# Four gate projections moved between the head pairs, five latent projections moved beside the triangular inverse

## The chip, the core and the metric

The kernel runs on one core of a Trainium2 chip. The metric is the device time of one execution in microseconds (us); lower is better. The engines are named as in the profile: PE is the matrix engine (PEld its weight loads, which overlap with it), DVE the vector engine, ACT the scalar engine, POOL the general engine, SP the engine that issues nearly all DMAs here. Every engine works off its own instructions in a fixed order; semaphores tie the orders together.

## What is computed

One layer of an encoder over 784 tokens (16 shared meta tokens, a prompt of 512 and a sample of 256). After a layer norm, one input projection feeds two branches; their outputs are concatenated, projected, normed, and put through a feed-forward block of width 4096.

```python
proj = h @ w_in                      # 1024 features -> 22 tiles of 128 columns
c_q, c_kv, k_r, qkv, z, a_f, a_b, b_f, b_b = split(proj)
q = rms_norm(c_q) @ w_uq             # latents of the attention: c_q 384, c_kv 256 columns
k, v = rms_norm(c_kv) @ w_uk, rms_norm(c_kv) @ w_uv
mla_out = softmax_attention(q, k, v)
qkv = silu(conv4(qkv))               # gated delta rule, both directions, 8 heads
m = strictly_lower((k*beta) @ k.T * decay)          # per chunk of 64 tokens
sol = solve(m + eye, ...)            # unit triangular, 112 matrices
o = scan over chunks (state S);  o = rms_norm(o) * silu(z)     # z: the gate, 512 columns
h = layer_norm(alpha*h + concat(mla_out, o) @ w_out)
h = layer_norm(alpha*h + relu(h @ w_ff1)**2 @ w_ff2)
```

## The kernel before

**Input projection.** `proj(ti)` makes one tile of 128 projected columns for all tokens. It loads 512 KB of weights (`wr`), splits them into a rounded part and a rest (`wh` by ACT, `wl` by DVE or POOL, chosen by `eng`), and issues 48 matmuls (8 feature tiles, 3 products, 2 halves of the tokens, 384 or 400 wide) into one of the two double banks `d2` of PSUM (`bank2()`). The weight tiles have two buffers each. There are 22 tiles: 0 holds the rotary keys and the decay gates; 1 to 8 are k and q of the four head pairs, in turns; 9 to 12 are v; 13 to 16 are the output gate z; 17 and 18 are the latents of k and v, 19 to 21 those of q.

**Pair stage.** `for j in range(NPB)` takes the four pairs in turn. `conv` projects k, then q, copies the result to `xb` and convolves it back into the same PSUM double bank (`y = ps...` where `wi < 8`). It stays there until `silu_pad` reads it with Silu. Then come the norms `l2` (Ln, Exp), the transposes `tokens`, the decay matrices `dc` and `en` (loads `x3` from `gD`, Exp), and the products that fill `LT` and the DRAM tile `UD`. ACT has to change its table between Silu and Ln/Exp. `act` puts the table load in place and orders it in the source's order: a load comes after every earlier activation of the other set. So pair j+1's Silu comes after all of pair j's Ln and Exp, and pair j+1's Ln after its own k's and q's Silu.

**First inverse.** `LT` is transposed (L585) and copied by DVE to `LP` (L587). `inv_steps` (L596, L598) then does 30 dependent steps of two DVE instructions each. The loop at L714 puts four such steps ahead of each of the eight tiles v0 to v3 (`vtok`) and z0 to z3 (`zgate`). `zgate` projects, applies Silu from PSUM to an SBUF tile, and stores that to `zD`; nobody reads `zD` before `finish`, in the delta rule. v is convolved into SBUF.

**Second inverse, latents, delta rule, attention.** The rest of the inverse (L724 to L775) ends in the stores to `tD`. Then `lat()` is a generator: its first part projects the five latent tiles and norms those of k and v, its next 18 parts are the up-projections (L657, L680, L704), one of them for each unit of the delta rule's loop (L904). Attention, output projection and feed-forward follow. Attention's pools and PSUM tiles lie where the inverse's and `lat()`'s lay, so it begins after both.

The framework's planner fixes every engine's order ahead of time. It runs the program through a model of the chip and gives an engine the earliest instruction in the source that is ready by that model; so later work moves ahead into idle places as far as its buffers are free, and the order doesn't change on the chip.

Of the kernel before, what the change touches and what calls it, by code (L numbers as in the profile page):

```python
# [5 lines left out]
F32 = mybir.dt.float32  # L6
# [10 lines left out]
NT = NM + NA + NB          # 784 unique tokens  # L17
NR = NA + NB               # 768 real tokens
KT = D // P                # 8 feature tiles
HT = NT // 2               # 392  # L20
HR = NR // 2               # 384
H0 = NT - HR               # 400
NCH = 14                   # 64-token chunks: A meta, A x8, B meta, B x4
GC = NCH * 64              # 896
NPB = 4                    # head pairs
# [59 lines left out]
def lay(inp):  # L85
    """host side: only places the inputs."""
    a = {}
    a["x"] = np.concatenate([inp["meta_tokens"], inp["x_prompt"][0], inp["x_sample"][0]], 0)
    w = inp["w_in"][0]
    cq, ckv, kr, q, k, v, z, g = (np.s_[0:384], np.s_[384:640], np.s_[640:672], np.s_[672:1184],  # L90
                                  np.s_[1184:1696], np.s_[1696:2208], np.s_[2208:2720], np.s_[2720:2752])
    tiles = [np.concatenate([w[:, kr], w[:, kr], w[:, g], np.zeros((D, 32), w.dtype)], 1)]
    for j in range(4):
        tiles.append(w[:, k][:, j * 128:(j + 1) * 128])
        tiles.append(w[:, q][:, j * 128:(j + 1) * 128])
    for s in (v, z, ckv, cq):
        t = w[:, s]
        for j in range(t.shape[1] // 128):
            tiles.append(t[:, j * 128:(j + 1) * 128])
    # [tile, p, k, 128]  # L100
    a["w_in"] = np.stack([t.reshape(KT, P, 128).transpose(1, 0, 2) for t in tiles])
    cols = [inp["ln_in_g"].reshape(8, 128).T, inp["ln_in_b"].reshape(8, 128).T]
    cols.append(inp["ln1_g"][0].reshape(8, 128).T)
    cols.append(inp["ln1_b"][0].reshape(8, 128).T)
    cols.append(inp["g_cq"][0].reshape(3, 128).T)
    cols.append(inp["g_ckv"][0].reshape(2, 128).T)
    cols.append(np.tile(inp["gdn_norm_g"][0], 2)[:, None])
    cols.append(inp["conv_w"][0].reshape(4, 12, 128).transpose(2, 1, 0).reshape(128, 48))
    a["cols"] = np.concatenate(cols, 1)
    a["gates"] = np.concatenate([inp["a_log_f"][0], inp["a_log_b"][0], inp["dt_bias_f"][0], inp["dt_bias_b"][0]])[None]  # L110
    a["rows"] = np.stack([inp["ln_in_g"], inp["ln_in_b"], inp["ln1_g"][0], inp["ln1_b"][0], inp["ln2_g"][0], inp["ln2_b"][0]])
    u = inp["w_uq"][0].reshape(384, 8, 96)
    t = []
    for h in range(8):
        n, r = u[:, h, :64], u[:, h, 64:]
        sw = np.concatenate([r[:, 16:], r[:, :16]], 1)
        t.append(np.concatenate([n, r, sw] if h % 2 == 0 else [r, sw, n], 1))
    a["w_uq"] = np.stack([x.reshape(3, 128, 128).transpose(1, 0, 2) for x in t], 1)   # [p, h, 3, 128]
    a["w_uk"] = inp["w_uk"][0].reshape(2, 128, 512).transpose(1, 0, 2)
    a["w_uv"] = inp["w_uv"][0].reshape(2, 128, 512).transpose(1, 0, 2)  # L120
    a["w_out"] = inp["w_out"][0]
    a["w_ff1"] = inp["w_ff1"][0].reshape(KT, P, FF // P, P).transpose(2, 1, 0, 3)    # [ft, p, k, 128]
    a["w_ff2"] = inp["w_ff2"][0]
    a["consts"] = _C
    a["rope"] = rope_tables()
    return {n: np.ascontiguousarray(v) for n, v in a.items()}
# [11 lines left out]
def body(ctx, tc, I, O):  # L138
# [10 lines left out]
    def banks_set(**bufs):  # L149
        """the eight banks, cut anew: name=number of tiles, of two banks where the name ends in 2."""  # L150
        want = list(bufs.items())
        n = 0
        while n < min(len(cut), len(want)) and cut[n][0] == want[n]:
            n += 1
        while len(cut) > n:
            (m, _), es = cut.pop()
            es.close()
            del banks[m]
        for m, b in want[n:]:
            es = ExitStack()  # L160
            banks[m] = es.enter_context(tc.tile_pool(name=f"ps_{m}", bufs=b, space=PSUM, reuse_waits="tile"))
            cut.append(((m, b), es))
# [15 lines left out]
    # activation table sets, switched in groups  # L178
# [31 lines left out]
    def split(src, hi, lo, eng=None):  # L210
        """hi + lo = src."""
        S.copy(hi, src)  # L212
        return (eng or V).tensor_sub(lo, src, hi.bitcast(F32))  # L213
# [3 lines left out]
    def moments(x, n, out, sp_):  # L217
        """mean and variance of the rows of x."""
# [5 lines left out]
    def norm_factors(m2, mv, sp_):  # L224
        """mv[..., 0] = -mean * rstd, mv[..., 1] = rstd from the mean and variance in m2[..., 2]."""
# [35 lines left out]
    bds = []  # L261
    for i in range(2):
        b = cvp.tile([P, 7, P], F32, name=f"bd{i}")
        G.memset(b, 0.0)
        bds.append(b)
# [54 lines left out]
    def proj(ti, real=False, wr=None, eng=V):  # L320
        """psum halves of projection tile ti: tokens 0..399 (16..399) and 400..783."""
# [71 lines left out]
    # gathered to [(h', s), dir, tile, parity, pair]  # L393
# [15 lines left out]
    # rows of gc (both directions) and -beta (forward), one line per (h', pair, chunk)  # L409
# [14 lines left out]
    egk = gqp.tile([P, 2, NCH, 4], F32, name="egk")      # exp(gc)  # L424
    act(egk, gcT, AF.Exp)
    ekd = gqp.tile([P, 2, NCH, 4], F32, name="ekd")      # exp(gl - gc)
    V.tensor_sub(ekd, glT, gcT)
    act(ekd, ekd, AF.Exp)
    egl = gqp.tile([P, 2, NCH, 4], F32, name="egl")      # exp(gl), natural head order
# [3 lines left out]
    # rotated keys, common to the heads  # L433
# [9 lines left out]
    ltp = pool(ctx, "ltp", 1, "left")  # L443
    LT = ltp.tile([P, 2, 56, 64], F32, name="LT")
    UD = dp.tile([2, NCH, P, 4, 2, 64], F32, name="UD")     # q, attention of a chunk
    vD = dp.tile([NCH, P, 4, 2, 64], F32, name="vD")        # k, v
# [5 lines left out]
    def conv(ti, wi, eng=V, ceng=V):  # L452
        """convolved projection tile (before silu), [128, 803]: A at 0, B at 531."""
# [19 lines left out]
    sp = pool(es, "sp", 1)  # L473

# [27 lines left out]
    def tokens(src, kt, j, w, mk):  # L502
        """src [(head, channel), chunks] by tokens to field w of the pair's k, v."""
# [21 lines left out]
    for j in range(NPB):  # L525
# [7 lines left out]
        for half in range(2):  # L533
# [3 lines left out]
            # rows of gc (both directions), -beta; of gc with the heads swapped  # L537
# [6 lines left out]
            # -beta decay, decay (forward); -beta decay, decay (backward)  # L544
# [13 lines left out]
            for a, w in ((0, 4), (4, 3)):  # L558
# [11 lines left out]
                for r in range(2):  # L570
                    st(UD[r, n0 + a:n0 + a + w, :, j].rearrange("n p i c -> p n (i c)"), ua[:, r, :w].rearrange("p n i c -> p n (i c)"))
    es.close()
    vp = pool(ec, "vp", 1)

    ei = ExitStack()
    ip = pool(ei, "ip", 1, "left")
# [24 lines left out]
    def lat():  # L601
# [1 line left out]
        def latent(t0, n, real, width, gn):  # L603
            cuts = ((NM if real else 0, H0), (H0, NT))
            a0 = cuts[0][0]
            raw = []
            sq = ml.tile([P, NT], F32, name="lsq")
            for i in range(n):
                ps = proj(t0 + i, real=real, eng=(V, V, V, G, G)[t0 + i - 17])
                r = ml.tile([P, NT], F32, name="lr", bufs=3)  # L610
                for s, (c0, c1) in enumerate(cuts):
                    S.copy(r[:, c0:c1], ps[:, s, :c1 - c0])
                if i == 0:
                    S.activation(sq[:, a0:], r[:, a0:], AF.Square)
                else:
                    s2 = ml.tile([P, NT], F32, name="ev", bufs=2)
                    S.activation(s2[:, a0:], r[:, a0:], AF.Square)
                    G.tensor_add(sq[:, a0:], sq[:, a0:], s2[:, a0:])
                raw.append(r)
            yield None  # L620
# [12 lines left out]
            yield res  # L633
# [10 lines left out]
        lk, lq = latent(17, 2, False, 256, "gckv"), latent(19, 3, True, 384, "gcq")  # L644
        next(lk)
        ck = next(lk)
        next(lq)
        yield
        halves = ((0, H0), (H0, NT))
# [42 lines left out]
        cq = next(lq)  # L692
        tq = ml.tile([P, NT], F32, name="lr", bufs=3)[:, :NR]
# [20 lines left out]
    for j in range(2 * NPB):  # L714
# [4 lines left out]
        else:  # L719
            zgate(j - NPB)  # L720
# [20 lines left out]
    for n0, r in ((0, 0), (96, 1), (16, 0), (80, 1), (32, 0), (64, 1), (48, 0), (56, 1)):  # L741
# [33 lines left out]
        st(tD.rearrange("p d n j c -> p (d n j) c")[:, ns], LTn[:, ns])  # L775
    el2 = ExitStack()
    ml = pool(el2, "ml", 1, "left")
    mv_ = pool(el2, "mv", 1, "left")
    latg = lat()
    next(latg)  # L780
    e1.close()

    # the chunk matrices are in DRAM by now: their place serves again
# [30 lines left out]
    def unit_a(c, step):  # L814
# [8 lines left out]
        # k exp(gc), v; q, attention, exp(gl), k exp(gl - gc)  # L823
# [107 lines left out]
    ei.close()  # L931
# [132 lines left out]
    def h1_half(s):  # L1064
        """normed tokens of one half, transposed; then scaled by rows for the residual."""
# [139 lines left out]
```

## Time and profile before

| | |
|---|---|
| median of 3 runs | 1242.83 us (1242.46 to 1246.13) |
| span of the profiled execution | 1241.3 us |
| instructions | 18703 |
| PE busy | 1168.4 us, 94% |
| DVE busy | 717.2 us, 58% |
| ACT busy | 511.2 us, 41% |
| POOL busy | 171.8 us, 14% |
| mean granted TensorE clock | 0.973 of full speed |

The span is the time from the first to the last instruction of one execution; the median of the runs lies 1.5 us above it. Busy shares are averages over stages with quite different limits, so the stages have to be read one at a time.

### The profile page before, as it was taken

Reading aid. Unit: us, or ns where it says so; the run is one execution under the profiler, and the core shown is the slowest. Engines: PE = TensorE matmul, PEld = TensorE weight load, DVE = VectorE, ACT = ScalarE, POOL = GpSimd, SP = SyncE. Lnnn points to the kernel's source line nnn. Section 1 sums busy time; section 2 is a strip of 40 time slices with the busy share of each in tenths; the row PEclk is TensorE's granted clock in tenths of the full one; section 3 lists DMA queues with packets and bytes.
Section 4 is the critical chain, followed back from the end, with each engine's and each line's share of the span. In section 5 each row is a group of like instructions: output and inputs, shape, how many; then the busy total and the mean of one; then the engine's idle time right before and its main releaser. Section 6 shows DMA issues by size and latency. Waiting matters only on the chain.

```text
span 1241.3 us, 18703 instructions
## 1 busy us (share of the span) xinstructions
PE 1168.4 (94%) x7468; PEld 1021.7 (82%) x7468; DVE 717.2 (58%) x1136; ACT 511.2 (41%) x974; POOL 171.8 (14%) x201
## 2 busy tenths in 40 slices
PE   5978879998999999989999899999999999999995
PEld 4867879998889877756758798989898989899994
DVE  8567668697967867684456584334243424343348
ACT  5475655324645666563545521203030303121113
POOL 2144554024223221020100000000000000000000
PEclk9888899999999999999999899999999999999998
DMA  5147764522497845340210230303030303131002
GB/s 202 50 111 182 183 166 142 122 92 90 143 268 220 250 132 137 124 140 31 93 52 35 85 102 30 106 24 114 1 119 17 119 18 102 35 100 36 1 1 102
DMA packets 92202, 126.49 MB, mean 102 GB/s; under 512 B 34946, under 2 KB 63362, under 8 KB 92114
## 3 DMA queue, kind: packets, MB, share of 16 engines
q1 hardware_dynamic: 92114, 125.28, 33.9%
q8 instruction: 59, 0.97, 0.3%
q14 instruction: 29, 0.24, 0.1%
HBM read 98.73 MB, written 26.53 MB: 101 GB/s over the span
## 4 chain that ended last, share of the span: by engine, by line
PE 78%; DVE 9%; DMA 5%; ACT 3%; issue 2%; SPq 1%; POOL 1%; DVEq 0%; ACTq 0%; POOLq 0%
PE d L1061 21%; PE b L1167 21%; PE d L331 7%; PE b L1103 5%; DMA x<-gD 3%; PE v L1000 3%; PE c L1003 3%; PE d L969 3%; PE d L704 2%; PE b L837 2%; PE b L853 2%; PE b L877 2%; PE b L870 2%; DVE LP L598 1%; DVE tm L596 1%
## 5 line engine op out<-in xcount | busy, mean ns | idle before, releaser
L1061 PE MATMUL d<-h1h,w1h 128*128 128x384 f32 x512 | 171.5, 337 | 1.3 <-ACT LT L1142 1.3
L1061 PE MATMUL d<-h1l,w1h 128*128 128x384 f32 x512 | 172.0, 336 | 0.0
L1061 PE MATMUL d<-h1h,w1l 128*128 128x384 f32 x512 | 171.9, 336 | 0.0
L1167 PE MATMUL b<-w2l,fh 128*128 128x512 f32 x384 | 151.3, 394 | 0.0
L1167 PE MATMUL b<-w2h,fh 128*128 128x512 f32 x384 | 150.5, 392 | 0.0
L1167 PE MATMUL b<-w2h,fl 128*128 128x512 f32 x384 | 147.6, 389 | 0.0
L1171 DVE TENSOR_TENSOR acc<-acc,b 128x512 f32<-128x512 f32 x84 | 55.9, 685 | 137.9 <-PE b L1167 137.9
L331 PE MATMUL d<-hTh,wl 128*128 128x384 f32 (+1 forms) x352 | 124.7, 354 | 4.2 <-DVE wl L213 4.2
L331 PE MATMUL d<-hTh,wh 128*128 128x384 f32 (+1 forms) x352 | 125.5, 356 | 2.1 <-ACT ks L188 2.1
L212 ACT CAST w2h<-LT 128x1024 fp32r<-128x1024 f32 x32 | 31.9, 1045 | 230.9 <-PE b L1167 212.3
L331 PE MATMUL d<-hTl,wh 128*128 128x384 f32 (+1 forms) x352 | 125.9, 358 | 0.1
L1061 PEld LDWEIGHTS d<-h1h,w1h 128*128 128x128 f32 x512 | 96.3, 189 | 2.7 <-ACT LT L1142 1.6
L1061 PEld LDWEIGHTS d<-h1l,w1h 128*128 128x128 f32 x512 | 96.7, 189 | 0.9 <-DVE h1l L213 0.3
L1061 PEld LDWEIGHTS d<-h1h,w1l 128*128 128x128 f32 x512 | 96.7, 189 | 0.6 <-DVE w1l L213 0.3
L213 DVE TENSOR_TENSOR w1l<-LT,w1h 128x1024 fp32r<-128x1024 f32 x32 | 39.2, 1224 | 88.9 <-ACT w1h L212 88.7
L1167 PEld LDWEIGHTS b<-w2h,fl 128*128 128x128 f32 x384 | 72.1, 188 | 16.1
L1167 PEld LDWEIGHTS b<-w2h,fh 128*128 128x128 f32 x384 | 72.1, 188 | 15.9
L1167 PEld LDWEIGHTS b<-w2l,fh 128*128 128x128 f32 x384 | 72.2, 188 | 13.7
L212 ACT CAST w1h<-LT 128x1024 fp32r<-128x1024 f32 x32 | 33.5, 1050 | 100.3 <-PE d L1061 100.2
L331 PEld LDWEIGHTS d<-hTh,wl 128*128 128x128 f32 x352 | 68.3, 194 | 6.7 <-DVE wl L213 4.6
L331 PEld LDWEIGHTS d<-hTh,wh 128*128 128x128 f32 x352 | 68.1, 193 | 6.7 <-issue 3.4
L331 PEld LDWEIGHTS d<-hTl,wh 128*128 128x128 f32 x352 | 68.1, 193 | 2.9 <-issue 1.5
(316 smaller groups left out, 2265.6 us busy)
## 6 DMA issues: line engine op xcount, KB each, us to landing
LT<-in_w_ff SPq DMA_DIRECT2D x64, 512.0 KB, 3.3
wr<-in_w_in SPq DMA_DIRECT2D x22, 512.0 KB, 3.3
x<-gD SPq DMA_DIRECT2D x16, 560.0 KB, 5.6
KV<-vD SPq DMA_DIRECT2D x26, 256.0 KB, 4.4
U<-UD SPq DMA_DIRECT2D x26, 256.0 KB, 5.2
UD<-ua SPq DMA_DIRECT2D x16, 256.0 KB, 5.1
wor<-in_w_out SPq DMA_DIRECT2D x8, 512.0 KB, 6.5
TB<-tD SPq DMA_DIRECT2D x52, 64.0 KB, 2.5
```

The costliest lines, as they stand in the source:

```text
L212: S.copy(hi, src)
L213: return (eng or V).tensor_sub(lo, src, hi.bitcast(F32))
L331: T.matmul(ps[:, s, :c1 - c0], lhsT=a[:, k, :], rhs=b[:, k, c0:c1], start=(k == 0 and i == 0), stop=(k == KT - 1 and i == 2))
L704: T.matmul(ps[:, s, :HR], lhsT=a[:, k], rhs=b[:, cs], start=(k == 0 and i == 0), stop=(k == 2 and i == 2))
L837: T.matmul(ps[:, j * P:(j + 1) * P], lhsT=TB[:, j], rhs=KV[:, j], start=True, stop=True)
L969: T.matmul(ps[:, :w], lhsT=q[:, qs], rhs=kt[:, k0:k0 + w], start=True, stop=True)
L1000: T.matmul(ps[:, t * P:(t + 1) * P], lhsT=p[:, c0:c0 + P], rhs=dg, start=True, stop=True)
L1003: T.matmul(po[:m, :nq], lhsT=Vs[j][:, t0 + bi, :m], rhs=pt[:, :nq], start=(bi == 0), stop=(bi == ntl - 1))
L1061: T.matmul(ps[:, s, :HR], lhsT=a[:, k, :], rhs=b[:, k, s * HR:(s + 1) * HR], start=(k == 0 and i == 0), stop=(k == KT - 1 and i == 2))
L1103: T.matmul(ps, lhsT=x[:, k, :], rhs=y[:, cs], start=(k == 0 and i == 0), stop=(k == 3 and i == 2))
L1167: T.matmul(ps, lhsT=a[:, qs], rhs=b[:, cs], start=(f == 0 and i == 0), stop=(f == NG - 1 and i == 2))
L1171: V.tensor_add(acc[:, ti, cs], acc[:, ti, cs], ps)
```

## The change

Besides removed comments the diff does four things. `zgate(j)` is called at the end of each pair's turn. The projections of the five latent tiles leave `lat()` and become `latraw(i)`, called in the loop of the first inverse after the four v tiles, where z stood; their raw results and sums of squares get tiles of their own (`lraw`, `lsqs`), which live until the up-projections end. `lat()`'s pools move to the right side of SBUF, opened after the projection's tiles (`hTh`, `hTl`, the weights) are given back, and the inverse's own pool is given back before `lat()` starts. The block matrices `bds` move to the pair stage's pool.

```diff
-    bds = []                                   # in pool cvp
+    bds = []                                   # the same, in pool sp
...
                     st(UD[r, n0 + a:n0 + a + w, :, j]...)
+        zgate(j)
     es.close()
     vp = pool(ec, "vp", 1)

+    elr = ExitStack()
+    lrp = pool(elr, "lrp", 1, "left")
+    lraw = [lrp.tile([P, NT], F32, name=f"lr{i}") for i in range(5)]
+    lsqs = [lrp.tile([P, NT], F32, name=f"lsq{i}") for i in range(2)]
+    def latraw(i):
+        real = i >= 2
+        ps = proj(17 + i, real=real, eng=(V, V, V, G, G)[i])
+        r, sq = lraw[i], lsqs[real]
+        a0 = NM if real else 0
+        for s, (c0, c1) in enumerate(RHALVES if real else HALVES):
+            S.copy(r[:, c0:c1], ps[:, s, :c1 - c0])
+        if i in (0, 2):
+            S.activation(sq[:, a0:], r[:, a0:], AF.Square)
+        else:
+            s2 = ytile()[:, :NT]
+            S.activation(s2[:, a0:], r[:, a0:], AF.Square)
+            G.tensor_add(sq[:, a0:], sq[:, a0:], s2[:, a0:])
...
         def latent(t0, n, real, width, gn):
-            raw = []
-            sq = ml.tile([P, NT], F32, name="lsq")
-            for i in range(n):
-                ps = proj(t0 + i, real=real, ...)    # and copy, square, add
-            yield None
+            raw = lraw[t0:t0 + n]
+            sq = lsqs[real]
...
-        lk, lq = latent(17, 2, False, 256, "gckv"), latent(19, 3, True, 384, "gcq")
-        next(lk)
-        ck = next(lk)
-        next(lq)
+        ck = latent(0, 2, False, 256, "gckv")
         yield
...
-        cq = next(lq)
-        tq = ml.tile([P, NT], F32, name="lr", bufs=3)[:, :NR]
+        cq = latent(2, 3, True, 384, "gcq")
+        tq = ml.tile([P, NT], F32, name="tq")[:, :NR]
...
-    for j in range(2 * NPB):
+    for j in range(NPB + 5):
         for _ in range(4):
             next(gi, None)
         if j < NPB:
             vtok(j)
         else:
-            zgate(j - NPB)
+            latraw(j - NPB)
...
+    e1.close()
     el2 = ExitStack()
-    ml = pool(el2, "ml", 1, "left")
-    mv_ = pool(el2, "mv", 1, "left")
+    ml = pool(el2, "ml", 1)
+    mv_ = pool(el2, "mv", 1)
+    ei.close()
     latg = lat()
     next(latg)
-    e1.close()
...
     el2.close()
-    ei.close()
+    elr.close()
```

## Rows read from the trace of the kernel before

**Rows 1.** Busy time by stretch: engines, granted clock, DMA share, GB/s.

```profile
60.00:205.00 145.00, 122.67 (x637) 112.42 (x636) 101.49 (x115) 90.40 (x156) 73.83 (x57) 0.89 0.64 156
205.00:302.30 97.30, 94.01 (x558) 92.81 (x556) 79.55 (x99) 34.81 (x57) 18.81 (x30) 1.00 0.36 97
302.30:360.00 57.70, 52.87 (x1110) 48.71 (x1111) 39.77 (x57) 35.81 (x61) 20.33 (x33) 0.91 0.59 193
360.00:647.00 287.00, 280.23 (x2032) 212.88 (x2030) 189.82 (x401) 166.08 (x430) 47.76 (x55) 0.99 0.47 138
647.00:1241.00 594.00, 573.70 (x2880) 517.28 (x2880) 266.17 (x377) 153.79 (x206) 0.00 (x0) 0.99 0.18 61
```

**Rows 2.** Timeline of ACT, table loads and Silu: start, us, instruction, [idle before].

```profile
68.01 1.28 ACT L184 ACT_TABLE_LOAD   x1
...
88.28 1.28 ACT L184 ACT_TABLE_LOAD   x1
89.57 0.90 ACT L188 ACTIVATE ks<-d 128x528 f32<-128x528 f32 x2
...
105.50 0.90 ACT L188 ACTIVATE ks<-d 128x528 f32<-128x528 f32 x2 [11.96 <-DVE d L465]
106.41 1.28 ACT L184 ACT_TABLE_LOAD   x1
...
126.86 1.28 ACT L184 ACT_TABLE_LOAD   x1
128.15 0.90 ACT L188 ACTIVATE ks<-d 128x528 f32<-128x528 f32 x2
131.70 0.90 ACT L188 ACTIVATE ks<-d 128x528 f32<-128x528 f32 x2 [2.65 <-DVE d L465]
132.62 1.28 ACT L184 ACT_TABLE_LOAD   x1
...
155.35 1.28 ACT L184 ACT_TABLE_LOAD   x1
...
170.86 1.28 ACT L184 ACT_TABLE_LOAD   x1
...
193.86 1.28 ACT L184 ACT_TABLE_LOAD   x1
```

**Rows 3.** Waits from 60 to 205 us: total, times, longest.

```profile
DVE dc L547 <- DMA x<-gD: 23.0, 7, 6.4
...
PE b L507 <- ACT kt L508: 7.2, 2, 4.6
```

**Rows 4.** The chain that ended last, 60 to 330 us: a projection run.

```profile
242.39 20.08 PE d L331 x113
```

**Rows 5.** Timeline of ACT, the steps from a projected tile to its Silu (q0).

```profile
61.67 0.48 ACT L457 COPY xb<-d 128x400 f32<-128x400 f32 x1
...
62.84 0.94 ACT L462 ACTIVATE d<-xb,cols 128x803 f32<-128x803 f32 x1
...
67.09 0.90 ACT L188 ACTIVATE ks<-d 128x528 f32<-128x528 f32 x2 [1.95 <-DVE d L465]
```

**Rows 6.** Stores of z, over the whole span.

```profile
L523 SPq DMA_DIRECT2D zD<-y x4: 320/326/568, 227.7 to 255.7; - x4
```

**Rows 7.** Timeline of DVE: last product into LT, first and last inverse step.

```profile
204.31 0.55 DVE L566 TENSOR_TENSOR LT<-b,dc 128x384 f32<-128x384 f32 x1
...
230.92 0.38 DVE L596 TENSOR_TENSOR tm<-LP 112x120 f32<-112x120 f32 x1
...
301.99 0.28 DVE L598 TENSOR_TENSOR LP<-LP,tm 112x120 f32<-112x120 f32 x1
```

**Rows 8.** Line L704 alone, by stretch: PE and PEld busy, clock, DMA.

```profile
360.00:400.00 40.00, 22.49 (x110) 18.29 (x108) 1.00 0.86 238
```

**Rows 9.** Instructions on tile wl: duration ns min/median/max.

```profile
L213 DVE TENSOR_TENSOR wl<-wr,wh x15: 1211/1227/3130, 51.5 to 263.6; 128x1024 fp32r<-128x1024 f32 x15
L213 POOL TENSOR_TENSOR wl<-wr,wh x7: 2347/2395/3247, 12.7 to 280.8; 128x1024 fp32r<-128x1024 f32 x7
```

More of the change, by code (lines that the diff above doesn't have):

```diff
@@ L260, in body @@
     cvp = pool(ec, "cvp", 1)
-    bds = []
[L262 to L265, printed above, removed]
     xbs = []
@@ L473, in body @@
     sp = pool(es, "sp", 1)
+    bds = []
+    for i in range(2):
+        b = sp.tile([P, 7, P], F32, name=f"bd{i}")
+        G.memset(b, 0.0)
+        bds.append(b)
     def silu_pad(y, ks):
@@ L571, in body @@
                     st(UD[r, n0 + a:n0 + a + w, :, j].rearrange("n p i c -> p n (i c)"), ua[:, r, :w].rearrange("p n i c -> p n (i c)"))
+        zgate(j)
     es.close()
     vp = pool(ec, "vp", 1)
+    elr = ExitStack()
+    lrp = pool(elr, "lrp", 1, "left")
+    lraw = [lrp.tile([P, NT], F32, name=f"lr{i}") for i in range(5)]
+    lsqs = [lrp.tile([P, NT], F32, name=f"lsq{i}") for i in range(2)]
+    HALVES = ((0, H0), (H0, NT))
+    RHALVES = ((NM, H0), (H0, NT))
+    def latraw(i):
[11 more added lines that the diff above has]
+            G.tensor_add(sq[:, a0:], sq[:, a0:], s2[:, a0:])
     ei = ExitStack()
@@ L603, in latent @@
         def latent(t0, n, real, width, gn):
-            cuts = ((NM if real else 0, H0), (H0, NT))
+            cuts = RHALVES if real else HALVES
             a0 = cuts[0][0]
-            raw = []
-            sq = ml.tile([P, NT], F32, name="lsq")
-            for i in range(n):
[L609 to L619, printed above, removed]
-            yield None
+            raw = lraw[t0:t0 + n]
+            sq = lsqs[real]
             for s, (c0, c1) in enumerate(cuts):
@@ L632, in latent @@
                 split(r[:, a0:], h[:, a0:], l[:, a0:], eng=V)
-            yield res
+            return res
         def load_u(src, n, w):
@@ L642, in load_u @@
             return wh, wl
-        lk, lq = latent(17, 2, False, 256, "gckv"), latent(19, 3, True, 384, "gcq")
-        next(lk)
-        ck = next(lk)
-        next(lq)
+        ck = latent(0, 2, False, 256, "gckv")
         yield
-        halves = ((0, H0), (H0, NT))
+        halves = HALVES
         for j in range(NPB):
```

## Prediction

> **What bounds the kernel now.** I read the busy time by stretch first. From 360 us on PE is busy for 280.23 of 287 us and for 573.70 of 594 us, at a granted clock of 0.99 [rows 1]: that part is PE's work, and an instruction that PE doesn't have to do there any more shortens it. From 205 to 302.3 us PE is busy for 94.01 of 97.30 us at full clock, and DVE for 79.55. Two things end there together: PE's projections, and DVE's chain of inverse steps, which runs from 230.92 to 302.27 us [rows 7]. Only between 60 and 205 us, the pair stage, is there room on PE: 122.67 busy of 145 us at a clock of 0.89 [rows 1], so at least 22 us idle.
>
> The timeline of ACT shows what paces that stage [rows 2]. A Ln/Exp phase of a pair runs from a table load to the next: 68.0 to 88.3, 106.4 to 126.9, 132.6 to 155.4, 170.9 to 193.9 us, that is 20.3, 20.5, 22.7 and 23.0 us. Between them lie Silu gaps of 18.1, 5.8 and 15.5 us, 39.4 in all. In a gap ACT waits for q to be convolved (11.96 us idle before the Silu at 105.50). In a phase the waits show why it is long: DVE waits 23.0 us in seven places for the loads of `x3`, PE 7.2 us in two places for a copy of ACT [rows 3].
>
> **The moved work.** A projection is 48 matmuls. 113 of them in an unbroken run take 20.08 us [rows 4], 0.178 us each, so 8.5 us a tile, and 34 us for the four of z. Before, z is stored between 227.7 and 255.7 us [rows 6], inside the stretch in which PE is full. No instruction of this is removed or added; the latents keep their 5 x 8.5 = 43 us and the planner already ran them in that stretch, so the latents' own move is nearly nothing: it only puts in the source the order that the trace has. What the change really does is to take 34 us of PE out of a full stretch and put it into one with 22 us idle.
>
> Z also brings into the pair stage four weight loads, four casts on ACT, two splits on DVE and two on POOL, four Silus and four stores on SP's queue. A split takes 1.23 us on DVE and 2.4 us on POOL by the median, up to 3.13 and 3.25 [rows 9]. DVE is busy for 101.49 of the stage's 145 us and POOL for 73.83 [rows 1], so 2 x 1.2 and 2 x 2.4 us fit, if not for nothing: at the longest rows it is 6.3 and 6.5 us. I count 0 to 6 us for the four, and take 2 us, because the splits are ready ahead of their matmuls. Table loads stay at the same number, since z's Silu stands next to the following pair's.
>
> The Trainium skill, "GPSIMD Engine Reference", Key points, says that GpSimd shares its SBUF interfaces with VectorE and contends with DVE instructions that have two SBUF inputs. The split's row agrees, as its longest DVE instance is 2.5 times the median; by that rule z's splits would cost more in the pair stage, where POOL is busier, than beside the inverse, and the sum would go by the upper bound of 6 us instead of 2.
>
> **The new wait.** This is what decides. The two double banks hold what ACT hasn't yet read. Before, while pair j is in its Ln/Exp phase, both k and q of pair j+1 are projected and convolved in PSUM, and the next gap can be short: 5.8 us at the second [rows 2]. Now z_j stands ahead of k_{j+1} in the source and takes the first bank that comes free. Its Silu may only run after all Ln and Exp of pair j. So in the phase z_j and k_{j+1} hold both banks, and q_{j+1} gets one only in the gap, after z_j's Silu. Queued behind are q's convolution, its Silu, the table load, and with them the pair's whole next phase.
>
> A gap then is in series: a table load, 1.3 us; z_j's Silu, 0.9 (by k's row); q's 48 matmuls, 8.5; copies, convolution and Silu, 61.67 to 67.99 = 6.3 us [rows 5]; in all 17 us. PE also has pair j's last products to do there and DVE its `LT` and `ua`; the first gap before, where the same works met, was 18.1 us. I take 20 us a gap, between 17 and 24. Three gaps of 20 us are 60, less 39.4 before: 20.6 us more, between 12 and 33. Against that stands that the phases get shorter: the loads of `x3`, 23.0 us of waits in seven places [rows 3], are issued by the time of the pair before, and land in the longer gap. I take a third of it back, 8 us, between 0 and 12. With the splits' 2 us the stage grows by 20.6 - 8 + 2 = 15 us (I call this D). From below PE itself sets a floor: the 34 us less 22 idle is 12, less what the clock gives back; 0.11 of the 145 us is 16 us of lost clock, some of it in the idle time. So D is between about 2 and 33.
>
> The Trainium skill, "PSUM — Partial Sum Buffer", Summary: rules for kernel authors, says to evacuate promptly, since PSUM is small. The gap at 5.8 us agrees with it from the other side, as there nothing else sat in the two banks; by that rule the gate should not wait in PSUM for a table, and the sum would go by the slower rival below.
>
> **What the pair stage's length does to the end.** From the last product into `LT` (204.86) to the first inverse step are 26 us, the steps take 71.3 [rows 7], and the second inverse until PE is full again at about 360 us takes 57.7 [rows 1]. This chain, 155 us, hangs on the pair stage's end and moves by D. It gets a little shorter: PE no longer has z to put between the transposes, and the second inverse meets less of `lat()`. I take 5 us for that (0 to 10: 4.8 us of PE idle in the last stretch and about as much lost to its clock of 0.91).
>
> The gain is that the place of z's 34 us in the inverse is free. The latents end earlier by it, and the up-projections of `lat()`, which now run as late as 400 us, move in. But only what stands after 360 us counts, and there is nothing else that could move ahead, because attention needs the places of the inverse and of `lat()`. After 360 us L704 has 110 matmuls left [rows 8]; at 0.178 us they are 19.6 us. So the rest, which is bound by PE, gets shorter by 19 us at most. `lat()`'s new place is that of `hTh` and `hTl`, so it can't begin before the last latent tile; that costs a hole of some 5 us on PE inside DVE's chain, where it is covered (if DVE's chain were not the longer one, it would be 5 us of the gain). I take 18 us, between 10 and 19.
>
> **The sum.** 15 (D) - 5 (chain) - 18 (up-projections) = -8 us. The span of 1241.3 becomes 1233; with the 1.5 us by which the runs' median lies above it, 1235 us.
>
> **Rivals.** *The gate fills idle places and nothing waits* (chance 0.20). If the planner lets q go ahead of z, or the gaps are hidden by the phases, D is near its floor of 2: 2 - 7 - 19 = -24, 1219 us. For it speaks that the idle 22 us and the low clock are there; against it that the order of the source and of the table loads forbids it.
>
> *The gate's hold on PSUM costs more than it frees* (0.24). Gaps of 24 us and phases no shorter: D = 33, 33 - 2 - 19 = +12, 1255 us. It becomes slower than before from D = 24 on, which is one long gap more. For it speaks that the gap at 105.50 was 18.1 us long although q had been projected before; against it the `x3` loads.
>
> *No change in the time* (0.12). With D = 23 the stage gives back what the up-projections gain: 1242. That also holds if the planner lets z slip behind the pairs, so that the source's new order doesn't appear in the trace.
>
> *The forecast* has the remaining 0.44, with its own range of 1226 to 1242.
>
> **How the numbers follow.** 0.3% is about what a measurement of this kernel can tell from no change, so faster is below 1239.1 and slower above 1246.6 us. Of the forecast's 0.44 some 0.36 lies below 1239.1, and 0.08 in the middle; with the first rival's 0.20 faster is 0.56. The middle gets 0.08 + 0.10 = 0.18, and slower 0.24 + 0.02 = 0.26. The range reaches from 1217, just under the first rival, to 1254, just under the second's end: what is left out on either side is about a tenth.
>
> **What would show it.** In the changed kernel's trace z's stores should lie between 90 and 215 us, right behind z's Silu and the table load. The q projections of pairs 1 to 3 should start after those Silus, with gaps of about 20 us each and phases under 21. The last product into `LT` should come at about 220 us instead of 204.86, the last inverse step at about 314, and L704 should be done when PE gets full, before 370 us. PE's granted clock between 60 us and the stage's end should be above 0.89. The prediction is wrong if q is projected before z's Silu (then too slow), if the gaps pass 24 us (then too fast), or if up-projections still run after the second inverse.

## The result and the profile after

The change made the kernel slower: 1316.19 us (1313.26 to 1319.60, 4 runs) against 1243.09 us (now 4 runs), a ratio of 1.058 with a 95% interval of 1.056 to 1.060. The forecast was 1235 us, its range ended at 1254, and it was to become faster. The page of the kernel after, busy time and the shares of the chain that ended last:

```profile
span 1314.8 us, 18783 instructions
PE 1192.8 (91%) x7468; PEld 1037.3 (79%) x7468; DVE 716.2 (54%) x1136; ACT 513.9 (39%) x974; POOL 176.3 (13%) x201
PE 67%; DVE 12%; DMA 8%; ACT 5%; issue 4%; POOL 2%; SPq 2%; DVEq 0%; POOLq 0%; ACTq 0%
```

The stretches of [rows 1], in the kernel after (PE, PEld, DVE, ACT and POOL busy, granted clock, DMA share, GB/s):

```profile
60.00:205.00 145.00, 126.89 (x657) 117.38 (x656) 80.59 (x96) 81.13 (x133) 65.64 (x53) 0.93 0.63 157
205.00:302.30 97.30, 90.90 (x532) 86.78 (x531) 79.50 (x90) 43.35 (x79) 26.88 (x34) 0.98 0.35 87
302.30:360.00 57.70, 47.20 (x549) 42.62 (x549) 44.82 (x58) 28.32 (x45) 14.15 (x11) 0.85 0.34 111
360.00:647.00 287.00, 240.58 (x2264) 189.81 (x2262) 170.12 (x346) 136.32 (x338) 48.42 (x72) 0.91 0.49 140
```

In the first row PE is busier than before, at a higher clock. Most of the loss stands in the last: where PE had been busy for 280.23 of 287 us, it now has 240.58, at a clock of 0.91 instead of 0.99. Two things reach that stretch, a late start and a hole. First the start. ACT's timeline, table loads of the pair stage (as [rows 2]), and the stores of z over the span (as [rows 6]):

```profile
67.36 1.28 ACT L184 ACT_TABLE_LOAD   x1
88.01 1.28 ACT L184 ACT_TABLE_LOAD   x1
89.31 0.81 ACT L188 ACTIVATE y<-d 128x768 f32<-128x768 f32 x1
...
111.04 0.90 ACT L188 ACTIVATE ks<-d 128x528 f32<-128x528 f32 x2 [6.51 <-DVE d L460]
111.96 1.28 ACT L184 ACT_TABLE_LOAD   x1
...
128.37 1.28 ACT L184 ACT_TABLE_LOAD   x1
...
154.82 1.28 ACT L184 ACT_TABLE_LOAD   x1
171.78 1.28 ACT L184 ACT_TABLE_LOAD   x1
197.29 1.28 ACT L184 ACT_TABLE_LOAD   x1
213.39 1.28 ACT L184 ACT_TABLE_LOAD   x1
```

```profile
L523 SPq DMA_DIRECT2D zD<-y x4: 450/524/584, 90.9 to 215.7; - x4
```

The Silu gaps are 24.0, 26.4 and 25.5 us, 75.9 in all instead of 39.4; the four phases add up to 70.1 us instead of 86.5. So the last table load comes 19.5 us later. DVE's timeline carries that on (as [rows 7]), and so do the stores of the second inverse's result `tD`, L775 before and L782 after:

```profile
224.57 0.54 DVE L566 TENSOR_TENSOR LT<-b,dc 128x384 f32<-128x384 f32 x1
...
251.99 0.37 DVE L619 TENSOR_TENSOR tm<-LP 112x120 f32<-112x120 f32 x1
...
331.63 0.28 DVE L621 TENSOR_TENSOR LP<-LP,tm 112x120 f32<-112x120 f32 x1
```

```profile
L775 SPq DMA_DIRECT2D tD<-LT x8: 373/570/1246, 329.7 to 358.0; - x8
```

```profile
L782 SPq DMA_DIRECT2D tD<-LT x8: 319/322/745, 361.6 to 393.2; - x8
```

The delay grows along the chain: 20.3 us at the last product, 21.1 at the first inverse step, 29.6 at the last step, 35.2 at the last store of tD. The hole is in the attention. Its exponentials (tile `p`: count, duration in ns min/median/max, first and last start), in the kernel before and after, and the state products of the delta rule's longest chain (L877 before, L885 after):

```profile
L188 ACT ACTIVATE p<-d,mx x48: 458/684/712, 412.4 to 625.9; 128x512 f32<-128x512 f32 x32, 128x256 f32<-128x256 f32 x16
```

```profile
L188 ACT ACTIVATE p<-d,mx x48: 465/686/705, 548.3 to 699.4; 128x512 f32<-128x512 f32 x32, 128x256 f32<-128x256 f32 x16
```

```profile
L877 PE MATMUL b<-YZ,XAf x128: 222/222/270, 398.4 to 529.3; 128*64 128x64 f32 x128
```

```profile
L885 PE MATMUL b<-YZ,XAf x128: 222/222/369, 432.2 to 536.1; 128*64 128x64 f32 x128
```

Before, the first exponential ran at 412.4 us, beside the delta rule, whose last state products start at 529.3; after, none runs until the delta rule is through. What held it shows one step ahead of the exponentials. The attention's score products on PE, and DVE's maxima `mx` of them, before and after:

```profile
L969 PE MATMUL d<-kt,q x96: 377/592/697, 410.2 to 624.8; 128*128 128x512 f32 x64, 128*128 128x256 f32 x32
L971 DVE TENSOR_REDUCE mx<-d x48: 406/681/693, 411.4 to 625.2; 128x1 f32<-128x512 f32 x32, 128x1 f32<-128x256 f32 x16
```

```profile
L977 PE MATMUL d<-kt,q x96: 379/592/697, 424.7 to 697.3; 128*128 128x512 f32 x64, 128*128 128x256 f32 x32
L979 DVE TENSOR_REDUCE mx<-d x48: 412/682/693, 536.9 to 697.7; 128x1 f32<-128x512 f32 x32, 128x1 f32<-128x256 f32 x16
```

Before, the first maximum follows the first score product by 1.2 us, after by 112.2 us: the scores of 424.7 us stand in PSUM, and the first tile that they need in SBUF comes only when the delta rule is done. From the last exponential to the end both kernels take 615.4 us, so the whole loss of 73 us is made by then: 35 us stand there when the second inverse ends, and the rest comes with two stages that no longer overlap.

### The profile page after: what moved, and what is told of

It is laid out like the page before. It is cut to its first block, busy times and chain, and to the rows that moved or that the text cites. A ratio compares the mean times of both kernels' runs of the same rounds, so it can differ in the third digit from the quotient of the medians.

```text
span 1314.8 us, 18783 instructions
## 1 busy us (share of the span) xinstructions
PE 1192.8 (91%) x7468; PEld 1037.3 (79%) x7468; DVE 716.2 (54%) x1136; ACT 513.9 (39%) x974; POOL 176.3 (13%) x201
## 4 chain that ended last, share of the span: by engine, by line
PE 67%; DVE 12%; DMA 8%; ACT 5%; issue 4%; POOL 2%; SPq 2%; DVEq 0%; POOLq 0%; ACTq 0%
PE d L1069 20%; PE b L1175 20%; PE b L1111 5%; PE d L326 5%; DMA x<-gD 3%; PE c L1011 3%; PE v L1008 3%; PE d L977 2%; DVE tm L619 2%; DVE LP L621 2%; PE d L711 2%; PE b L845 1%; PE d L664 1%; DVE YZ L865 1%; DMA kt<-KD 1%
## 5 line engine op out<-in xcount | busy, mean ns | idle before, releaser
L1175 PEld LDWEIGHTS b<-w2h,fl 128*128 128x128 f32 x384 | 72.1, 188 | 16.1
```

The lines of the kernel that those rows point to most:

```text
L1175: T.matmul(ps, lhsT=a[:, qs], rhs=b[:, cs], start=(f == 0 and i == 0), stop=(f == NG - 1 and i == 2))
```

## The experiments

All times are medians of at least four runs; each kernel is compared with runs of the kernel before on the same chip (1242 to 1243 us).

**The two parts apart.** The gate alone (the kernel before plus `zgate(j)` at the end of each pair), and the latents alone (the whole change, gate back behind v):

```diff
 e1:  +        zgate(j)             # end of each pair; out of the inverse's loop
 e2:  -        zgate(j)             # out of the pair stage
      +        elif j < 2 * NPB:    # loop of the inverse: v, z, then latraw
      +            zgate(j - NPB)
```

> The kernel before with one edit: the four gate tiles are projected at the end of each pair's turn instead of behind the v tiles; the latents and all pools stay as before. Two theories of the 73 us. Theory A (places in SBUF): the pair stage's 20 us are only a part, and the larger part comes from the new places of the pools, which keep the delta rule's loads waiting for the second inverse and attention's tiles waiting for the delta rule. Then this kernel has the 20 us longer pair stage, gets some of it back from the up-projections, and takes 1245 to 1265 us. Theory B (the gate's hold on the double banks): the longer pair stage shifts and disorders everything behind it, and this kernel takes 1290 us or more, like the changed one.

> The changed kernel with the gate tiles put back behind the four v tiles, ahead of the five latent tiles; the latents' own tiles and the new places of all pools stay as changed. Theory A (places): no pair-stage loss, but the loss behind the second inverse stays: 1285 to 1305 us, with the first KV load of the delta rule after the end of the second inverse and attention's value matmuls after the delta rule. Theory B (the gate's hold): 1238 to 1250 us, as before.

Gate alone: 1273.18 us, ratio 1.024 [1.021, 1.027], +30 us. Latents alone: 1298.28 us, 1.045 [1.042, 1.047], +55 us, with the pair stage as before (last table load at 193.3) and the last store of `tD` at 354.9 us, 3 us earlier than before, so that none of e2's loss is a late chain. So e1 fits neither of its theories (8 us above A's range, far below B's), and e2 fits A. Both parts lose, and the part that I had costed at nothing loses more.

**Where the delta rule's tiles lie.** The right side of SBUF is a stack. `lat()`'s pools opened there first take 48,832 bytes a partition (46,784 of `ml`, 2,048 of `mv`, by the tiles' sizes), so `up` and `uz`, opened next, move down by as much; by the program's layout they then lie over the inverse's `gs` and over the attention's tiles for exponentials, their transposes and maxima. Both can be a wait: KV and U for the second inverse, the exponentials for the delta rule. e3 puts `lat()`'s tiles on the left again in the whole change, fitted by single buffers of `ur` and `ul`; e4 adds a copy that takes the gate out of PSUM at once; e6 keeps e2's layout but makes `ml` 7,232 bytes smaller, which clears `gs` and not the attention; e5 is e2 with the tiles on the left.

```diff
 e3, e5: -    ml = pool(el2, "ml", 1)
         +    ml = pool(el2, "ml", 1, "left")    # above ip; ur, ul bufs=1; tq = lraw[0]
 e4:     +        S.copy(z[:, :NR]..., ps[:, :, :HR])    # then Silu on z in place
 e6:     +        tq = lraw[0][:, :NR]                   # ur, ul bufs=1, ml stays on the right
```

> The changed kernel with lat()'s pool on the left side again, above the inverse's pool, and made to fit there (one buffer instead of two for the raw and the low part of the up-projection weights; the table of the rotation takes the place of the first raw latent), so that the delta rule's pools get their place of before. Gates and latents are projected where the change puts them. Theory A: the KV loads start before the inverse ends, attention overlaps with the delta rule again, and the time falls to 1240 to 1265 us. Theory B: it stays above 1290 us.

> The kernel of the third run with one more edit: ACT copies the gate's projection out of PSUM as soon as it is there, and the Silu later works on the copy in SBUF; four copies more, about 0.8 us each. If the gate's hold on a double bank makes the Silu gaps 25 us long, q's projection no longer waits for the gate's Silu, the three gaps get shorter by 5 to 10 us each, and the time is 10 to 25 us below the third run's. If the gaps are long because of DVE's convolution or the loads, nothing changes by more than 4 us.

> The gate is where it was before (behind v); the five latent projections stay in the first inverse, behind the gate, with raw results apart; the latents' tiles lie on the left of SBUF above the inverse's, so that the delta rule's tiles lie where they lay before. Theory A (the latents' part cost its 55 us by the places of the delta rule's tiles): 1233 to 1250 us, first KV load before 300 us, scores of the attention from 400 us on. Rival B (the latents in the inverse cost it themselves, by waits in the inverse or in the up-projections): above 1275 us.

> As the latents-only kernel (latents' tiles on the right, gate behind v), but the latents' pool is 7232 bytes per partition smaller, so that the delta rule's lowest tile begins just above the inverse's topmost one (gs), while its state tiles still share their place with the attention's tiles for exponentials and maxima. Theory A1 (the late KV and U loads, which waited for the second inverse, are what costs): 1243 to 1265 us. A2 (the attention that can't start beside the delta rule is what costs): 1275 to 1300 us, first value product of the attention still behind the last product of the delta rule, although KV is loaded early.

| | us | ratio to before | first KV load | first exponential |
|---|---|---|---|---|
| before | 1242 to 1243 | 1 | 298.0 | 412.4 |
| whole change | 1316.19 | 1.058 | 391.4 | 548.3 |
| e3, on the left | 1275.86 | 1.027 [1.026, 1.029] | 295.5 | 441.4 |
| e4, and gate copied out | 1278.22 | 1.030 [1.026, 1.033] | 287.1 | 435.3 |
| e2, latents alone | 1298.28 | 1.045 | 353.9 | 527.4 |
| e6, `gs` cleared | 1297.36 | 1.044 [1.042, 1.045] | 297.1 | 529.5 |
| e5, latents on the left | 1274.60 | 1.025 [1.022, 1.029] | 293.2 | 454.0 |

The exponentials and the KV loads of e6, where the two suspects come apart:

```profile
L188 ACT ACTIVATE p<-d,mx x48: 457/686/734, 529.5 to 680.5; 128x512 f32<-128x512 f32 x32, 128x256 f32<-128x256 f32 x16
```

```profile
L835 SPq DMA_DIRECT2D KV<-vD x26: 422/594/1842, 297.1 to 480.4; - x26
```

KV comes 57 us earlier than in e2 and the time stays; the exponentials still wait for the delta rule's end. The maxima say the same: from the first score product to the first maximum it is 83.8 us in e2, 67.7 in e6 and 3.1 in e3. So the places cost by the attention, 40 us in the whole change (e3) and 24 in the latents' part (e2 against e5). The late loads cost nothing as long as the attention waits; what they would cost alone no run shows. e3 came 11 us above its range, and e5 fell between its two: on the left the latents still cost 31 us. e3 and e5 have single buffers of `ur` and `ul` besides, so if those cost anything, the places cost more than 40 and 24 us. e4 answers one of the prediction's rivals: with a gate that ACT copies out of PSUM during the phase, the gaps fall to 65.3 us in all, but the phases grow, and the time doesn't fall. The Trainium skill, "PSUM — Partial Sum Buffer", Summary: rules for kernel authors, says to evacuate promptly; here that was worth nothing by itself.

**The gate's price: dose and order.** e7 moves z0 and z1 only. e8 moves all four, but each behind q of the next pair, so that k and q take the two double banks first.

```diff
 e7: +        if j < 2: zgate(j)       # end of the pair; z2, z3 stay behind v
 e8:          yq = conv(2 + 2 * j, j, ...)
     +        if j: zgate(j - 1)       # z3 at the stage's end
```

> Kernel before with only z0 and z1 in the pair stage (behind pairs 0 and 1), z2 and z3 left behind v. Theory A (each gate tile is a plain addition to a stage that has no room for it, and was free beside the inverse): half of the 30 us, 1253 to 1264 us. Rival B (one tile in the stage finds idle places, only more of them cost): under 1249 us. Rival C (the first gate tile already sets the pace of every gap): 1266 to 1278 us.

> Kernel before with the gate tile of pair j projected behind q of pair j+1, not ahead of k (z3 at the stage's end), so that k and q take the two double banks first. Theory A (the prediction's: the gate ahead of q holds a bank and makes the gaps): gaps under 20 us, the stage's last table load before 204 us, 1247 to 1262 us. Rival B (what the gate adds is its work and its place in the chains of a stage without room, wherever it stands): last table load 208 to 216 us, 1266 to 1280 us.

e7: 1258.95 us, 1.013 [1.010, 1.015], half of the price. e8: 1253.51 us, 1.008 [1.005, 1.011], a third of it. ACT's timeline in e8:

```profile
89.89 1.28 ACT L184 ACT_TABLE_LOAD   x1
...
107.72 1.28 ACT L184 ACT_TABLE_LOAD   x1
125.79 1.28 ACT L184 ACT_TABLE_LOAD   x1
...
141.85 1.28 ACT L184 ACT_TABLE_LOAD   x1
163.80 1.28 ACT L184 ACT_TABLE_LOAD   x1
...
181.34 1.28 ACT L184 ACT_TABLE_LOAD   x1
200.64 1.28 ACT L184 ACT_TABLE_LOAD   x1
```

The gaps are 17.8, 16.1 and 17.5 us, 51.4 in all. So the prediction's new wait was there, and it is one of order: with the gate ahead of k and q instead of behind them, the gate alone costs 20 us more, of 30. Both came as their theories A said.

**What the freed place is worth.** e10 projects the gate tiles in both places; e11 projects them nowhere.

```diff
 e10: +        zgate(j)                # end of each pair, and behind v as before
 e11: -        ps = proj(13 + j, ...)
      +        act(z[:, :NR], hTh[:, j, NM:NT].bitcast(F32), AF.Silu)
```

> Kernel before with the four gate tiles projected twice: once at the end of each pair (as in the change) and once more behind v, where they stood. Against the gate-only kernel (1273 us) it has nothing but the 34 us of PE back in the first inverse. The prediction's view (the freed place there is worth 18 to 23 us): 1290 to 1297 us. Rival (the inverse is a chain of DVE and PE's work beside it was free): 1266 to 1281 us.

> Kernel before without the four gate projections: in their place Silu of four tiles of the normed input is stored, so 192 matmuls, their weight loads and splits are left out and the output isn't the reference's. The prediction's view (the place in the first inverse is worth 18 to 23 us when it is freed): 1219 to 1226 us. Rival (that work was free beside the inverse): 1235 to 1246 us.

e10: 1274.12 us, 1.025 [1.021, 1.028], within 1 us of e1, although PE has four tiles more to project there, some 34 us. e11, which stores Silu of the normed input as the gate: 1251.00 us (1243.35 to 1258.11), 1.007 [1.004, 1.009], 5 us above its rival's range: 192 matmuls fewer, and not faster. The windows from the first to the last inverse step point to why (length, then PE, PEld, DVE, ACT and POOL busy); in turn before, e10, e1, e11 and after:

```profile
230.80:302.30 71.50, 68.21 (x386) 67.19 (x385) 66.96 (x74) 24.13 (x36) 14.69 (x16) 1.00 0.31 87
```

```profile
251.80:320.20 68.40, 68.40 (x390) 67.71 (x389) 65.99 (x69) 21.33 (x31) 13.50 (x6) 1.00 0.34 93
```

```profile
250.30:327.20 76.90, 60.43 (x295) 55.20 (x293) 74.91 (x81) 32.47 (x56) 36.76 (x36) 0.87 0.29 86
```

```profile
227.20:308.40 81.20, 61.80 (x300) 56.01 (x299) 76.17 (x80) 32.38 (x57) 41.27 (x38) 0.81 0.36 99
```

```profile
251.90:332.00 80.10, 67.91 (x357) 61.26 (x356) 75.25 (x79) 29.79 (x51) 27.75 (x22) 0.89 0.28 78
```

DVE is busy for 94 to 97% of each of these windows, PE for 76 to 100%. The inverse is about as long as DVE's work in it. When the projections run out, the planner puts the next work that is ready beside the steps, in these kernels the latents' norms and splits, and DVE and POOL get more to do. The sixty step instructions themselves take longer as well; DVE's groups in the same window, before and after:

```profile
L598 DVE TENSOR_TENSOR LP<-LP,tm 112x120 f32<-112x120 f32 (+14 forms) x30 | 31.4, 1045 | 0.8
L596 DVE TENSOR_TENSOR tm<-LP 112x120 f32<-112x120 f32 (+14 forms) x30 | 27.1, 902 | 0.9
```

```profile
L619 DVE TENSOR_TENSOR tm<-LP 112x120 f32<-112x120 f32 (+14 forms) x30 | 33.4, 1114 | 0.9
L621 DVE TENSOR_TENSOR LP<-LP,tm 112x120 f32<-112x120 f32 (+14 forms) x30 | 30.0, 999 | 0.9
```

That is 63.4 instead of 58.5 us for the same steps, beside a POOL that is busy for 27.75 instead of 14.69 us; the other DVE work is 11.9 instead of 8.5 us. In the five windows the steps take 58.5 and 59.3 us where POOL is busy for 14.69 and 13.50 (before, e10), and 63.4, 64.0 and 64.9 where it is busy for 27.75, 36.76 and 41.27 (after, e1, e11). No run changed POOL's work alone.

**A version from the gaps.** In e8 the first gap was no longer than before, and the third 2 us longer. So z0 and z2 (e13), or z0 alone (e15), go behind q there, and the other tiles stay behind v. e12 was meant as e13, but its loop runs 24 of the inverse's 30 steps and leaves six out; its 1240.54 us (0.998 [0.996, 0.999]) is therefore no version.

```diff
 e13:         yq = conv(2 + 2 * j, j, ...)
      +        if j in (1, 3): zgate(j - 1)     # e15: j == 1 only
```

> Kernel before with z0 behind q of pair 1 and z2 behind q of pair 3, where the gaps were 18.1 and 15.5 us already and grew by 0 and 2 us with a gate tile behind q; z1 and z3 stay behind v. Theory A (a gate tile is free where the gap is long anyway): last table load before 197 us, 1236 to 1247 us. Rival B (two tiles cost by what they take out of the inverse, as the half dose did, +16 us): 1252 to 1264 us.

> Kernel before with z0 behind q of pair 1 and z2 behind q of pair 3, z1 and z3 behind v, and all 30 steps of the inverse (the run with two tiles before this one ran only 24 of them). Theory A (a gate tile is free where the gap is long anyway): last table load before 197 us and 1238 to 1247 us. Rival B (what two tiles take out of the first inverse lets work of the latents onto DVE there, as in the half dose): 1250 to 1262 us.

> Kernel before with z0 alone behind q of pair 1, in the gap that is 18.1 us long already; z1 to z3 behind v. Theory A: 1238 to 1246 us, no change or slightly faster. Rival B (each tile taken out of the inverse costs 4 us there): 1246 to 1252 us.

e13: 1247.05 us, 1.003 [1.002, 1.005], at the upper edge of A. e15: 1244.78 us, 1.001 [1.000, 1.003], within A. Tiles in long gaps are nearly free here, and nothing is gained elsewhere. No version that does all the work beats the kernel before.

**The latents' remaining 31 us.** In e5 the inverse ends 7 us earlier than before, yet the end is late. k's up-projections (L657 before, L663 in e5), before and in e5, and the window from 304 to 353 us, before and in e5:

```profile
L657 PE MATMUL d<-lh,uh x16: 332/347/1095, 297.8 to 326.2; 128*128 128x400 f32 x8, 128*128 128x384 f32 x8
```

```profile
L663 PE MATMUL d<-lh,uh x16: 337/528/702, 307.6 to 366.8; 128*128 128x400 f32 x8, 128*128 128x384 f32 x8
```

```profile
304.00:353.00 49.00, 44.20 (x1029) 40.33 (x1028) 36.97 (x51) 31.98 (x55) 17.72 (x27) 0.91 0.53 177
```

```profile
304.00:353.00 49.00, 42.84 (x923) 35.86 (x919) 38.72 (x59) 21.67 (x40) 9.22 (x16) 0.50 0.35 116
```

They start 10 us later, the last begins 41 us later, and PE runs the second inverse at a granted clock of 0.50. e14 puts the norm factor of the k and v latents right behind their two projections, as it ran before. e16 takes the loads of the up-projections' weights out of SP's queue, where in e5 a load of KV ahead of them waited from 261.8 to 293.3 us for the last projection (the first `ur` went out at 297.4 us, before at 256.6). e18 does both.

```diff
 e14: +            if j == 2 * NPB + 1: latnorm(False, 256)    # behind latraw(1)
 e16: -            ld(wr, src)
      +            nc.gpsimd.dma_start(wr, src)
```

> The kernel with the latents' tiles on the left and the gate behind v (1274.6 us), but the norm factor of the k and v latents (two sums over the features on PE, Ln, Exp) stands in the source right behind their two projections, ahead of the three of q's latents, as it did before the change. Theory A (the change put all five projections ahead of that norm, so the up-projections start late, meet the second inverse, and PE falls to half clock there): k's up-projections start before 303 us, clock from 310 to 360 us above 0.75, 1243 to 1262 us. Rival B (the up-projections wait for the places of their weights, which the convolution's y tiles hold until the last latent): within 6 us of 1274.6.

> The kernel with the latents' tiles on the left and the gate behind v (1274.6 us), but the loads of the up-projections' weights (ur) go out on POOL's queue instead of SP's, where in that kernel they stood behind KV's first load, which waited from 261.8 to 293.3 us for the place of the normed input; the first ur went out at 297.4 us instead of 256.6. Theory Q (that wait in SP's queue made the up-projections late): first ur before 275 us, k's up-projections start before 300 us, granted clock from 310 to 360 us above 0.8, 1240 to 1260 us. Rival P (uh and ul lie on the convolution's tiles, which are held until the last latent's square, so the weights can't be used earlier): within 6 us of 1274.6.

> The kernel with the norm of the k and v latents put early (1258.5 us), and the weights of the up-projections on POOL's queue. If the norm's order and SP's queue each have a half of the latents' 31 us: 1238 to 1250 us. If the weights' place holds them (rival P) or the norm's order had the same wait: 1252 to 1264 us.

e14: 1258.45 us, 1.013 [1.011, 1.014], 16 us less than e5 and inside A's range, but by luck: none of A's signs is there. The up-projections start at 313.6 us, the clock from 304 to 353 us is 0.53, and the last up-projection begins at 447.0 us, in e5 at 446.8. So the norm's early place is worth 16 us by a way that I don't know. e16: 1266.24 us, 1.019 [1.017, 1.020], between its two ranges, and e18: 1265.88 us, 1.018 [1.015, 1.022], above both of its. In both, the first `ur` went out later still, at 309.9 and 311.0 us, behind POOL's own work, so they don't test the queue of SP.

One rival is untested: all kernels with the tiles on the left have single buffers of `ur` and `ul`, which the whole change doesn't have. It can't explain the first `ur`, but it can explain some of the rest, as POOL's second split in e5 waits for the products that read the first (POOL's timeline, idle time in brackets):

```profile
334.87 0.72 POOL L213 TENSOR_TENSOR ul<-ur,uh 128x256 fp32r<-128x256 f32 x1 [8.79 <-PE d L663]
```

What is shown is that the up-projections come late and meet the second inverse at half clock. That this makes the 31 us isn't shown (e14 is 16 us faster with up-projections as late), and which order, place or buffer makes them late stays open.

**The mended change.** e9 is e3 with the gate behind q; e17 is e9 with the weights on POOL's queue.

> The whole change with both suspected faults taken out: the latents' tiles on the left, so that the delta rule's tiles lie where they lay before, and each gate tile behind q of the next pair. Theory A (places and the gate's order ahead of q are the two causes, and nothing else of the change costs): what the gate behind q costs alone, 1248 to 1260 us. Rival B (the latents' early projection with all norms behind it makes the up-projections late, which the longer pair stage only covered): the latents' own 31 us come out again, 1268 to 1282 us.

> The change with three faults taken out: latents' tiles on the left, gate behind q (together 1267.4 us), and the weights of the up-projections on POOL's queue. Theory Q: the 14 us that this kernel lay above the gate behind q alone go away, 1247 to 1259 us. Rival P: 1262 to 1273 us.

e9: 1267.37 us, 1.020 [1.017, 1.023], between its ranges, just below B's. e17: 1267.95 us, 1.020 [1.018, 1.022], within P's. With the gate's delay cut, part of the latents' own price comes out: 14 us above e8. So of the 73 us, 40 are places (after to e3), 8 the gate's order (e3 to e9), and 25 remain (e9 to before). The gate behind q costs 11 by itself (e8); the cause of the other 14 is open.

## Why the prediction was wrong

**"The latents' own move is nearly nothing."** This is the step that failed most: put at nothing, it cost 55 us by itself (e2). It looked at when the five projections run and not at where the new tiles lie. Its own sentence that the attention needs the places of the inverse and of `lat()` bounded the gain, but I didn't ask whose places the attention would need after the change: now the delta rule's. That is shown by e3, e5 and e6 and by the 112 us between scores and maxima, and costs 40 us of the change's 73. Of `lat()`'s new place I saw only the 5 us hole on PE. What the latents cost beside the places, 31 us in e5, stays open.

**"So the rest gets shorter by 18 us."** This failed too. Filling the gate's place in the inverse again cost 0.9 us (e10), and emptying it gained nothing (e11). The up-projections did move in: the last of L711 begins at 391.3 us, ahead of the last store of `tD` at 393.2, while before, the last of L704 began at 398.1 us, 40 us behind that store. But the stretch behind got longer instead of shorter, as the attention waited in it. [rows 1] had shown DVE at 79.55 of 97.30 us in the inverse; the reading that both ends come together there was right, and what follows from it by these runs is that taking PE's work out lets other work of DVE in.

**"It gets a little shorter", the chain, by 5 us.** It got longer by 15 us: 8.6 in the inverse's steps and 5.6 from there to the last store of tD, the rest ahead of the first step. The Trainium skill, "GPSIMD Engine Reference", Key points, which I weighed for the splits alone, says that POOL and DVE share SBUF interfaces; the windows above agree, with POOL busy for 27.75 instead of 14.69 us and the same steps 4.9 us longer, though no run shows that this is the cause. For the second inverse, 5.6 us longer, no run shows a cause either.

**D, 15 us.** The mechanism was right, z's Silu behind the table load and q behind z, and the size too small: 20.3 us, inside D's own bounds. The gaps were 75.9 us instead of 60, two of the three past the 24 us that I had named as the point where it goes wrong; the phases shrank by 16.3 us instead of 8, which covered part of the miss. The reason given for that was wrong: DVE waits for `x3` 23.1 us in seven places, as before [rows 3]. PE's clock from 60 to 205 us rose to 0.93, as expected.

**The rivals.** The second, a gate that costs more than it frees, went the right way for the gate's part, +30 us in e1, though with a D of 19 us (last product at 223.0) and not 33; what it left out is that the chain gets longer and the freed place gives nothing. It blamed the hold on PSUM; e4 speaks against the hold alone, e8 for the order in which z and q take the banks. The first rival is ruled out by the gaps, and "no change" by the time.

## What to carry to other kernels

When a change opens or reorders pools, work out every later pool's place before costing anything: two stages that overlapped can be made to run one after the other by tiles that neither of them changed. In a trace it shows as a result that stands ready while its first reader waits. PE's work beside the chain that DVE paces was free here, and taking it out let the planner fill the room with work that came with a longer chain. The order in which tiles ask for a scarce buffer can matter more than how long one holds it: in the whole change with its tiles on the left, the order was worth 8 us (e9), the early copy nothing (e4).

## What was not expected of the hardware

PE's granted clock can stay at its lower level, 1.2 GHz, while PE counts as busy: 0.50 over 49 us of e5 with 42.84 us of busy time, against 0.91 with 44.20 in the kernel before. Two stretches of each, before and e5:

```profile
302.00:306.00 4.00, 3.67 (x17) 3.66 (x18) 0.28 (x1) 2.48 (x3) 3.57 (x12) 0.59 1.01 356
330.00:342.00 12.00, 10.92 (x352) 10.35 (x345) 11.71 (x20) 5.17 (x8) 2.76 (x5) 1.00 0.69 224
```

```profile
302.00:306.00 4.00, 2.76 (x66) 2.28 (x66) 4.00 (x3) 3.94 (x7) 4.00 (x4) 0.59 0.06 14
330.00:342.00 12.00, 12.00 (x331) 10.96 (x327) 9.31 (x15) 5.22 (x9) 1.76 (x3) 0.50 0.58 213
```

In both the clock fell to half at about 303 us, behind four us in which PE was idle for much of the time (from 298 to 302 us it was busy for 1.01 us before and 2.33 in e5). Before, PE then ran products of k's up-projections in a row, and the clock was at 0.98 from 306 to 310 us. In e5 it ran the second inverse's 32x32 products with single up-projections between them, and the clock stayed at 0.50 until 354 us, also where PE was busy without a break. The same 32x32 products took 236 ns there instead of 191 by the median. What makes the clock return in the one and not in the other, these runs don't show.
